# Two-layer decoder trunk on one core: the second layer's latents as seven half-size products, and the sums of the fourth product of the last projection made ahead of its splits

## The chip, the core and the metric

The kernel runs on one core of a Trainium2 chip. The metric is device time in microseconds (us) for one execution of the whole program, lower is better. The kernel before has a median of 718.78 us over 3 runs (718.22 to 719.83). Engines are named as in the profile: PE is TensorE (PEld its weight loads), ACT is ScalarE, DVE is VectorE, POOL is GpSimd, SP is SyncE, which here only issues DMAs.

## The reference

512 tokens of width 1024 go through two layers and a last norm. What matters here is the second layer (multi-head latent attention):

```python
def mla_layer(x, cos, sin, norm_g, w_in, q_norm_g, w_q_b, kv_norm_g, w_kv_b, w_out):
    h = rmsnorm(x, norm_g)
    proj = h @ w_in                       # 512 x 1024 times 1024 x (384 + 256 + 64 + 2048)
    q_lat, kv_lat, k_rope, z = proj[..., :o1], proj[..., o1:o2], proj[..., o2:o3], proj[..., o3:]
    q = (rmsnorm(q_lat, q_norm_g) @ w_q_b).reshape(B, S, N_HEADS, QK_HEAD_DIM)
    kv = (rmsnorm(kv_lat, kv_norm_g) @ w_kv_b).reshape(B, S, N_HEADS, QK_NOPE_DIM + V_HEAD_DIM)
...
    o = causal_mla_attention(q_nope, q_rope, k_nope, k_rope, v)
    y = o.reshape(B, S, MLA_WIDTH) * jax.nn.silu(z)
    return x + y @ w_out                  # 512 x 2048 times 2048 x 1024
```

All is float32. The first 704 columns of proj (384 + 256 + 64) are called the latents here; the other 2048 feed the gates, silu(z).

## The kernel before

**Arithmetic.** A float32 product is made of three fast ones: every operand is split into a high half (`w_hi`, `h_hi`, `a_hi`: ScalarE copies it into the type fp32r) and a low half (what is left; VectorE or GpSimd subtracts). `mm3` (lines 183 to 185) multiplies high by high, low by high and high by low into one bank of PSUM. So each strip of weights costs a pass of ScalarE and then a pass of VectorE (or GpSimd) before TensorE can use it. `halves` (188, 189) does this for data, `strip` (166, 167) for weights loaded into five `raw` buffers, `Summed.strip` (559, 560) for weights that stand in tiles of their own. Halves of weights live in four buffers (`WB = 4`, tag "w"), so two strips at a time. PSUM has eight banks, given out by `bank()`.

**Seven products for eight.** Both output projections cut their matrices into two by two quarters and multiply by a scheme of Strassen's kind: seven products of sums of quarters take the place of eight. `x_sum` and `y_sum` hold sums of weight quarters, made by loads (some of them adding loads of GpSimd's queue); `s1`, `s2`, `s3`, `n3` are sums of token quarters, made by VectorE (`combine`, `combine_rows`, line 1055). `multiply` runs one product: two strips (q) by two tiles of 128 tokens (t), each of them `part`, 12 matmuls. `gather` (610) adds a bank to the residual `xs`.

**Around the latents.** The last product of the first layer's projection goes tile by tile; `norm_a` and `norm_b` (226: transposes through PSUM, then halves) make the second layer's normed tokens `h_hi`, `h_lo`, feature major. `lat_block(i, t)` then makes the latents without any scheme: two halves of 352 columns by two halves of the 1024 features (four strips, low halves on GpSimd) by four token tiles, 12 matmuls each. A bank is copied to `lat` (706). After that `latents()` norms them (rms of the 384 and of the 256 columns), and `gates(0)` to `gates(7)`, 48 matmuls of 512 columns each, run with the transposes of the latents, the rope of the keys and of the first queries between them.

**Order.** Here and in the attention the framework's planner sets the order of each engine's queue: an instruction that the program writes first goes first, unless its model of the work says that another is ready earlier; a tile of memory is handed on when its last reader is done. At the start and in the last projection, under `tc.manual_schedule()`, each engine takes its instructions in the order in which the program writes them.

**The last projection** (`products`, `finish`): seven products over `a11` to `a22`, quarters of `y`. Before `products`, the attention's last heads run the first one (into `acc`) and prepare the second. In `products`: second product (`t1`, into `both`), third (`p2`, into `last`), fourth (`y1` by `n3`, into `both`), fifth (`t2` by `s2`, into `acc`), sixth (`y2` by `s3`), and in `finish` the seventh (`t4` by `a22`).

## Time and profile before

| | |
|---|---|
| median of 3 runs | 718.78 us (718.22 to 719.83) |
| the profiled execution's own time | 719.61 us |
| its span, first to last instruction | 717.8 us |
| mean granted TensorE clock | 0.991 |
| instructions | 10049, of them 3529 matmuls |
| latents, starts of the first and the last matmul of 352 columns | 313.12 and 345.49 us |
| gates(0), starts of its first and last matmul | 345.65 and 356.33 us |
| last projection: second product starts, kernel ends | about 639 us, 717.8 us |

How to read the profile: times are from the start of the span. In the timeline a row is start, duration, engine, line, operation, written tile<-read tiles, shape and count; in brackets stands how long the engine was idle before it and what released it. A matmul's duration holds its way through the array, so the rate is read from the distance between starts. In the list of waits a row is who waited, for whom, total us, times, longest. Groups by shape give count, then busy us and mean ns of one. "Granted clock" is TensorE's share of its full clock.

## The change

**The latents.** `norm_b` gets a third argument: it turns both halves of a token tile first, makes the halves, and then ScalarE also copies the plain values from PSUM into `hf`, the upper half of the tile `y`, which the gates fill only later. `lat_block` gives way to `latent_products`: tokens are cut into two halves of 256, features into two halves of 512, columns into two of 352. Four quarters of weights are loaded into tiles of their own (`w_q`, eight loads of 352 KB) and added in place by VectorE; token sums are made in place in `hf`; seven products of 24 matmuls are accumulated in six banks and read out to `lat` by ScalarE and VectorE with the signs that the scheme asks. All low halves of these strips are VectorE's. `gates(0)` moves from behind the latents to between the second and the third product; `latents` (the norm) follows the products, and `gates(1)` stands where `gates(0)` stood, and so on.

**The last projection.** The third product's second strip moves up, ahead of two sums and of the two reads of `acc`; all of `n3` is summed before its first split; the two strips of the fourth product are written apart with the second split of `n3` between them; the reads of `acc` come after them.

```diff
-    def norm_b(t, xn):
-        for b in range(2):
-            pt = bank()
+    def norm_b(t, xn, plain=None):
+        pts = [bank() for _ in range(2)]
+        for b, pt in enumerate(pts):
...
+        if plain is not None:
+            for b, pt in enumerate(pts):
+                o = plain[:, 4 * b : 4 * b + 4, t * P : (t + 1) * P]
+                act.activation(o, pt.rearrange("p (k c) -> p k c", k=4), AF.Copy)
...
-    lat_block(0, 0)
-    norm_b(2, xn[2])
-    lat_block(0, 1)
-    lat_block(1, 0)
-    norm_b(3, xn[3])
-    for i, t in ((1, 1), (0, 2), (0, 3), (1, 2), (1, 3)):
-        lat_block(i, t)
-    for i in (2, 3):
-        for t in range(NT):
-            lat_block(i, t)
...
+        def form(raw):
+            hi = wp.tile([P, W], F32R, name="w_hi", tag="w", bufs=WB)
+            lo = wp.tile([P, W], F32R, name="w_lo", tag="w", bufs=WB)
+            hv, lv = (t[:, : 4 * HL].rearrange("p (k c) -> p k c", k=4) for t in (hi, lo))
+            for k in (slice(0, 2), slice(2, 4)):
+                halves(raw[:, k, :], hv[:, k, :], lv[:, k, :])
+            return hv, lv
+
+        def add(a, b):
+            for k in (slice(0, 2), slice(2, 4)):
+                dve.tensor_tensor(a[:, k, :], a[:, k, :], b[:, k, :], ALU.add)
...
+        p1 = form(b11)
+        times(acc, p1, tokens(0, 0), True, 0)
+        norm_b(2, xn[2], hf)
+        times(acc, p1, tokens(0, 0), True, 1)
+        p2 = form(b21)
+        times(last, p2, tokens(0, 1), True, 0)
+        norm_b(3, xn[3], hf)
+        times(last, p2, tokens(0, 1), True, 1)
+        add(b11, b12)
+        gates(0)
+        dve.tensor_tensor(a22, a21, a22, ALU.subtract)
+        s1 = a_form(a22, "one")
+        for t in range(2):
+            act.activation(lat[:, t, cl], acc[t][:, cols], AF.Copy)
+        both = [bank() for _ in range(2)]
+        t1 = form(b11)
+        product(both, t1, s1, True)
+        dve.tensor_tensor(a21, a11, a21, ALU.subtract)
+        dve.tensor_tensor(a11, a22, a11, ALU.subtract)
+        add(b11, b22)
+        s2 = a_form(a11, "two")
+        t2 = form(b11)
+        for t in range(2):
+            dve.tensor_tensor(lat[:, t, cl], lat[:, t, cl], last[t][:, cols], ALU.add)
+            act.activation(lat[:, 2 + t, cr], both[t][:, cols], AF.Copy)
+        product(acc, t2, s2, False)
+        dve.tensor_tensor(a12, a11, a12, ALU.add)
+        n3 = a_form(a12, "one")
+        y1 = form(b22)
+        for t in range(2):
+            act.activation(lat[:, t, cr], acc[t][:, cols], AF.Copy, scale=-1.0)
+        product(both, y1, n3, False)
+        add(b12, b22)
+        s3 = a_form(a21, "two")
+        y2 = form(b12)
+        for t in range(2):
+            dve.tensor_tensor(lat[:, t, cr], lat[:, t, cr], both[t][:, cols], ALU.add)
+        product(acc, y2, s3, False)
+        add(b11, b21)
+        t4 = form(b11)
+        for t in range(2):
+            c = lat[:, 2 + t, cr]
+            dve.tensor_tensor(c, c, acc[t][:, cols], ALU.subtract)
+        for t in range(2):
+            times(acc, t4, tokens(1, 1), False, t)
+            act.activation(lat[:, 2 + t, cl], acc[t][:, cols], AF.Copy)
...
         split_rows(a12, slots[1], 4, 8)
+        p2.append(y_sum.strip(1))
         combine_rows(s3, a11, a21, ALU.subtract, 6, 8)
         combine_rows(s2, s1, a11, ALU.subtract, 6, 8)
-        for t in range(2):
-            gather(t, LEFT, acc[t])
-        p2.append(y_sum.strip(1))
         y_sum.load(1, RIGHT)
         multiply(last, p2, slots[1], True)
         n3 = a12
-        combine_rows(n3, s2, a12, ALU.add, 0, 4)
+        combine_rows(n3, s2, a12, ALU.add, 0, 8)
         split_rows(n3, slots[0], 0, 4)
-        combine_rows(n3, s2, a12, ALU.add, 4, 8)
-        split_rows(n3, slots[0], 4, 8)
         for t in range(2):
             gather(2 + t, RIGHT, both[t])
-        y1 = y_sum.strips()
+        y1 = [y_sum.strip(0)]
+        split_rows(n3, slots[0], 4, 8)
+        y1.append(y_sum.strip(1))
+        for t in range(2):
+            gather(t, LEFT, acc[t])
```

## What was predicted, before the change was built

> **What bounds the kernel now.** I read the page first (shares, chain), then TensorE's list of waits, then a table of stages, then the timeline of the two places that the change touches.

> ```profile
> PE 701.5 (98%) x3529; PEld 600.8 (84%) x3529; DVE 444.5 (62%) x866; ACT 347.2 (48%) x748; POOL 138.0 (19%) x182
> ...
> PE 93%; DVE 3%; issue 1%; ACT 1%; DMA 0%; POOL 0%; POOLq 0%; SPq 0%; DVEq 0%; ACTq 0%
> ```

> TensorE is busy 98% of the span and carries 93% of the chain that ended last. So time falls only by fewer matmuls or fewer waits of TensorE.

> ```profile
> PE bank L183 <- ACT w_hi L559: 2.5, 1, 2.5
> ...
> PE bank L226 <- DVE xn L218: 0.6, 1, 0.6
> PE bank L185 <- DVE w_lo L560: 0.5, 1, 0.5
> ```

> Those are TensorE's only waits of 0.5 us or more once the first products run. The one of 0.6 us is for the second layer's norm and stays; the other two belong to the strips of the last projection.

> ```profile
> 313.00:357.00 44.00, 44.00 (x263) 41.71 (x261) 18.77 (x44) 23.02 (x59) 23.89 (x35) 1.00 0.40 111
> ...
> 660.40:670.30 9.90, 6.89 (x17) 4.64 (x16) 8.98 (x9) 6.57 (x7) 4.86 (x4) 0.66 0.31 50
> ```

> The columns are the stretch, its length, then busy time of PE, PEld, DVE, ACT and POOL, the granted clock, and DMA. The latents with gates(0) (313 to 357) have no idle PE, with VectorE at 18.77 of 44. Around 660 PE idles, and the clock is 0.66. The timeline shows it:

> ```profile
> 650.00 0.39 PE L184 MATMUL bank<-w_hi,a_lo 128*128 128x512 f32 x1
> ...
> 660.42 0.39 PE L185 MATMUL bank<-w_lo,a_hi 128*128 128x512 f32 x1
> 663.29 0.69 PE L183 MATMUL bank<-w_hi,a_hi 128*128 128x512 f32 x1 [2.48 <-ACT w_hi L559]
> 663.78 0.63 PE L184 MATMUL bank<-w_hi,a_lo 128*128 128x512 f32 x1
> 664.94 0.80 PE L185 MATMUL bank<-w_lo,a_hi 128*128 128x512 f32 x1 [0.52 <-DVE w_lo L560]
> ...
> 669.80 0.58 PE L184 MATMUL bank<-w_hi,a_lo 128*128 128x512 f32 x1
> 670.22 0.39 PE L185 MATMUL bank<-w_lo,a_hi 128*128 128x512 f32 x1
> ```

> From 650.00 to 660.42 lie 47 matmuls, 46 steps of 0.2265 us. From 660.42 to 670.22 there are 15 steps, 9.80 us; at 0.2265 they would be 3.40. The hole costs **6.40 us**: about 2.6 us of wait, 0.5 of a second one, and some 3.3 because the matmuls up to 669.80 come 0.43 us apart, at half clock, until it recovers.

> **Part 1, the latents: matmuls.** Before: 16 blocks of 12, 192 matmuls of 352 columns. After: seven products of 24, 168.

> ```profile
> 321.34 0.32 PE L183 MATMUL bank<-w_hi,h_hi 128*128 128x352 f32 x1
> ...
> 345.49 0.32 PE L185 MATMUL bank<-w_lo,h_hi 128*128 128x352 f32 x1
> ```

> This run has 153 rows, 152 steps: 0.1589 us each. The 24 that go are worth **3.81 us**. [...]

> **Part 1: what the seven products ask of VectorE.** Low halves of the strips now run on VectorE, and VectorE adds weights and tokens. Rows for the rates:

> ```profile
> 338.11 2.20 ACT L166 ACTIVATE w_hi<-raw 128x512 fp32r<-128x512 f32 x4 [5.13 <-PE bank L184]
> 661.20 3.88 ACT L559 ACTIVATE w_hi<-b_y 128x1024 fp32r<-128x1024 f32 x4
> 671.19 0.63 ACT L1219 ACTIVATE junk<-xs 128x512 f32<-128x512 f32 x1 [4.22 <-DVE xs L610]
> ...
> 671.94 0.63 ACT L1219 ACTIVATE junk<-xs 128x512 f32<-128x512 f32 x1
> 338.78 2.50 DVE L167 TENSOR_TENSOR w_lo<-raw,w_hi 128x512 fp32r<-128x512 f32 x4 [16.24 <-ACT w_hi L166]
> 663.66 4.62 DVE L560 TENSOR_TENSOR w_lo<-b_y,w_hi 128x1024 fp32r<-128x1024 f32 x4
> ```

> and, from the groups by shape in 313 to 357 (count, then busy us and mean ns):

> ```profile
> L189 DVE TENSOR_TENSOR h_lo<-bank,h_hi 128x512 fp32r<-128x512 f32 x5 | 3.3, 685 | 0.2 <-ACT h_hi L188 0.2
> L218 DVE SCALAR_TENSOR_TENSOR xn<-xs,rs,g_mla 128x1024 f32<-128x1024 f32 x2 | 2.6, 1285 | 4.6 <-POOL rs L204 4.6
> ...
> L610 DVE TENSOR_TENSOR xs<-xs,bank 128x512 f32<-128x512 f32 x1 | 0.7, 678 | 0.0
> ```

> Per operation in a row: VectorE 0.625 us at 512 columns, 1.155 at 1024, so 0.82 for the new shape of 704 (between those rows); ScalarE 0.55, 0.97 and so 0.71; a square with its sum takes 0.75. From the first product's start (313.1) to the last one's start VectorE has: 6 strips, two pieces each (9.8 us); the gates(0) strip (2.5); 4 weight sums of two pieces (6.6); 4 token sums (4.6); 4 low halves of tokens (4.6); 6 bank reads of 352 columns at some 0.46 (by the slope of the two rows; 0.625 at most), 2.8; and what it has already, 3.3 + 2.6 + 0.7. Sum 37.5 us. TensorE in the same stretch: 6 products (22.9), gates(0), 48 x 0.2265 = 10.9, and two norm transposes:

> ```profile
> 315.05 1.04 PE L226 MATMUL bank<-ident,xn 128*128 128x128 f32 x8
> 315.84 0.41 PE L183 MATMUL bank<-w_hi,h_hi 128*128 128x352 f32 x1
> ```

> 0.8 us each. Sum 35.4. VectorE's 37.5 drops by 2.2 for what is not in the way (one bank read, the last strip's second piece, the part of a norm that ran ahead of 313.1): 35.3 against 35.4. It is now as loaded as TensorE. Worked through in program order, gates(0) lets it make the sums for the next two products ahead; afterwards each product has 3.8 us of cover against 4.0 to 5.4 us of VectorE work, and TensorE is reached about the end. ScalarE's high halves must come first (0.71 for each piece), and strips wait for one of two pairs of weight buffers, free when the product before the last one ends. I take **1.0 us** of waits in all; bounds: 0 (every sum made ahead) and 4 (VectorE never idle in the sum above, but waiting about 0.8 us for ScalarE at each of five products). Below nothing it cannot go, since this stretch has no idle PE to win back. Latents net: 1.0 - 3.8 = **-2.8 us**.

> **At nothing.** The eight plain copies of the norm (ScalarE, 0.55 each) lie where ScalarE has 21 of 44 us free; uncovered, two would hold a norm's banks 1.1 us longer. gates(0) only moves: gates(1), 10.9 us, takes over hiding the latents' norm and the rows of it; the projection loads of gates(0) are queued on SP behind eight loads of quarter weights, which need memory of the first layer's last strips:

> ```profile
> 302.21 2.35 DVE L560 TENSOR_TENSOR w_lo<-b_x,w_hi 128x1024 fp32r<-128x1024 f32 x2
> ...
> raw<-in_mla_w_in SPq DMA_DIRECT2D x16, 176.0 KB, 2.5
> ```

> free by 304.6 at the latest; 352 KB at twice the 2.5 us are there by 310, and TensorE wants the product at 313.1. If that cover went, 2 to 3 us. GpSimd loses 16 low halves; nobody waited for them.

> **Part 2, the fourth product's operands.** What made the hole, in order on ScalarE and VectorE:

> ```profile
> 649.74 2.01 ACT L559 ACTIVATE w_hi<-b_y 128x1024 fp32r<-128x1024 f32 x2 [0.98 <-PE bank L184]
> 656.62 1.06 ACT L188 ACTIVATE a_hi<-y 128x1024 fp32r<-128x1024 f32 x1 [4.86 <-DVE y L1055]
> 660.23 1.06 ACT L188 ACTIVATE a_hi<-y 128x1024 fp32r<-128x1024 f32 x1 [2.56 <-DVE y L1055]
> ...
> 649.37 1.22 DVE L189 TENSOR_TENSOR a_lo<-y,a_hi 128x1024 fp32r<-128x1024 f32 x1
> 655.29 1.29 DVE L1055 TENSOR_TENSOR y<-y 128x512 f32<-128x512 f32 x2
> 657.71 1.23 DVE L189 TENSOR_TENSOR a_lo<-y,a_hi 128x1024 fp32r<-128x1024 f32 x1 [1.13 <-ACT a_hi L188]
> 658.85 1.29 DVE L1055 TENSOR_TENSOR y<-y 128x512 f32<-128x512 f32 x2
> 662.47 1.28 DVE L610 TENSOR_TENSOR xs<-xs,bank 128x512 f32<-128x512 f32 x2
> ```

> The second half of the sum waits on VectorE behind a low half that waits for ScalarE; ScalarE's queue then holds the strip (661.20) behind that sum's high half (660.23). New order: third product's second strip, low, from its first high half at 650.8 to 653.1; two sums to 654.4; all four pieces of n3 (0.64 each) to 657.0. ScalarE: first half of n3 from 655.7, at worst from 657.0; strip of y1 done by 658.6, at worst 659.9. VectorE: low half to 658.1, two reads of banks to 659.4, y1's first piece to 660.6. TensorE wants high halves at 660.65 and the first low at 661.1: no wait, 0.5 us to spare. Then n3's rest to 662.9 and y1's second strip to 665.2, wanted at 666.1. The moved reads of acc end at 666.5, s2's low halves 668.8, last's reads 670.1. ScalarE squares these (0.75 each) to 670.95, and only then takes the fifth product's strip: first high 671.5, first low 672.1; wanted 671.5 and 672.0. I keep 0.2 us of wait there: **-6.2 us**. Loads:

> ```profile
> b_y<-in_mla_w_out SPq DMA_DIRECT2D x4, 512.0 KB, 6.0
> ```

> y1's are issued as p2's low halves end (648.3 to 653.1) and wanted from 656.7 to 661.8, 8.4 us or more later, 6.0 needed. GpSimd's adding loads go earlier with them.

> Sum: 719.61 - 2.8 - 6.2 = 710.6 for a profiled execution; that one lies 0.83 above the median, which gives **709.8**.

> **Rivals.** (a) The forecast, 709.8: 0.63. (b) VectorE's load costs the latents all they save, in waits under 2 us each: 718.8 - 6.2 = 712.6. For it: 35.3 against 35.4; against: GpSimd's part is gone, and gates(0) lets work run ahead. 0.14. (c) The hole only moves to the fifth product, behind the squares (0.1 us to spare): 2.5 us of wait and the half clock are back, 718.8 - 2.8 = 716.0. 0.11. It needs 2 us of lateness that my queue does not have. (d) The half clock after the hole is not in every run. The lowest time is only 1.39 below the profiled one, so at most that much of 3.3 us is absent; the median gains 1.2 less: 711.0. 0.05. [...] (e) Slower: in the latents the sums queue behind each other so that two of the five late products wait 2.5 us or more. The hole shows the price of such a wait, 6.4 us with the clock: 718.8 - 10.0 + 12.8 = 721.6. It decides from 2.5 us on; for it, t2's step is 7.7 us of VectorE (two token sums, a weight sum, two low halves, two bank reads) against 3.8 of cover if gates(0) did not help. 0.05. No change within the bound: 0.02. That the change does not do as it says I see no room for: seven calls, one order written by hand.

> **How the numbers follow.** Low end: no waits (-3.8 - 6.4) and 0.6 of scatter: 708.0. High end: (a), (b), (d) and (b) with 2 us more, 714.8; (c) and (e) left out, 0.16 to 0.18. About 0.2% (1.4 us) is what a measurement here can tell from no change. Faster: a to d, 0.93, less 0.02 for mixtures: 0.91; same 0.04; slower 0.05.

> **What would show it.** Right: no wait of PE for the strip's high half near 660, clock 1.0 there, matmuls 0.2265 apart; 168 matmuls of 352 columns 0.159 apart; VectorE near full from 313 to 349; PE waits there of about 1 us in sum. Wrong: PE waits of 2 us or a clock below 1 among the products, or a new hole at the squares.

## The result, and the profile after

The change's median is 711.67 us over 4 runs (711.33 to 712.01), against 718.79 for the kernel before, run beside it. The ratio is 0.9896, with a 95% interval of 0.9884 to 0.9908. Its profiled execution took 712.01 us (span 710.2, clock 0.992), 7.60 less than that of before. Timed again later it gave 711.06 (710.38 to 711.35), 0.9882 (0.9869 to 0.9895). The forecast was 709.8, so the direction and the range held and the gain came out 1.9 us smaller.

From the page of the changed kernel, the engines' busy time and the shares of the chain:

```profile
PE 696.8 (98%) x3505; PEld 596.5 (84%) x3505; DVE 474.0 (67%) x902; ACT 358.4 (50%) x758; POOL 126.2 (18%) x166
...
PE 94%; DVE 2%; issue 1%; ACT 1%; POOL 1%; DMA 1%; POOLq 0%; SPq 0%; DVEq 0%; ACTq 0%
```

TensorE runs 24 matmuls less and is still the bound. Its list of waits, without those of the first 10 us:

```profile
PE bank L226 <- DVE xn L218: 0.9, 2, 0.6
PE bank L183 <- ACT h_hi L188: 0.4, 1, 0.4
PE bank L185 <- DVE h_lo L189: 0.4, 1, 0.4
```

The 2.5 us for the strip's high half and the 0.5 behind it are gone. Three waits are new: one of 0.3 for a norm (the 0.9 holds two waits, and the other, of 0.6, was there before), and two of 0.4 that name the halves of normed tokens. None names a strip of the late products. The windows of the two places (stretch, length, busy PE, PEld, DVE, ACT, POOL, granted clock, DMA):

```profile
313.00:353.00 40.00, 38.85 (x224) 35.85 (x223) 37.14 (x49) 28.13 (x54) 7.62 (x12) 1.00 0.13 41
...
651.00:662.00 11.00, 11.00 (x50) 9.13 (x49) 10.97 (x14) 6.53 (x7) 2.42 (x2) 1.00 0.63 212
```

VectorE, at 18.77 of 44 before, is now busy 37.14 of 40 in the latents, and PE has about 1.2 us without work there. Where the hole was, PE is full at clock 1.00. The timeline of the same place, the step into the fourth product:

```profile
659.12 0.39 PE L185 MATMUL bank<-w_lo,a_hi 128*128 128x512 f32 x1
659.35 0.39 PE L183 MATMUL bank<-w_hi,a_hi 128*128 128x512 f32 x1
659.58 0.39 PE L184 MATMUL bank<-w_hi,a_lo 128*128 128x512 f32 x1
659.80 0.39 PE L185 MATMUL bank<-w_lo,a_hi 128*128 128x512 f32 x1
```

The matmul of 659.12 is the third product's last and that of 659.35 the fourth's first; starts lie 0.22 to 0.23 apart across the step. The first low half was ready in time:

```profile
657.90 2.35 DVE L564 TENSOR_TENSOR w_lo<-b_y,w_hi 128x1024 fp32r<-128x1024 f32 x2
```

The first of its two pieces ends about 659.1, and the matmul that wants it starts at 659.80: 0.7 us to spare, where the prediction had 0.5.

**Where the 7.60 us are**, from starts of matmuls in the two profiled executions. The first matmul of 352 columns comes 0.63 later (313.12, then 313.75); the first one of 512 columns does too (26.31, then 26.93), so this was there before any line of the change had run, and 712.01 is the highest of the four runs. From the first 352-column matmul to the first transpose of the latents' rows, gates(0) and gates(1) both counted: 54.31, now 52.34, so 1.97 less. From there to the last product's last high matmul: 342.97, now 336.73, so 6.24 less. What is left is 0.02.

## The experiments

The table has those two stretches for each kernel's profiled execution ("latents", "after them"; gates(1), 48 x 0.2265 = 10.87 us, moved into the first where it stands later), beside the times. Ratios are against the kernel before, timed beside each.

| kernel | median us | ratio (95%) | latents | after them |
|---|---|---|---|---|
| before | 718.79 | 1 | 54.31 | 342.97 |
| the change | 711.67 | 0.9896 (0.9884 to 0.9908) | 52.34 | 336.73 |
| last projection only | 712.82 | 0.9923 (0.9910 to 0.9937) | 54.30 | 336.73 |
| latents only | 716.76 | 0.9973 (0.9959 to 0.9987) | 52.35 | 342.11 |
| two strips' low halves on GpSimd | 712.59 | 0.9924 (0.9909 to 0.9938) | 54.20 | 336.70 |
| plain copy first | 709.74 | 0.9881 (0.9866 to 0.9897) | 51.35 | 336.72 |
| reads of acc where they were | 710.65 | 0.9893 (0.9875 to 0.9911) | 52.35 | 336.89 |
| n3 by halves in turn | 714.42 | 0.9942 (0.9924 to 0.9960) | 52.35 | 339.65 |
| 8 spare sums | 717.87 | 0.9988 (0.9977 to 0.9999) | 58.69 | 336.72 |
| 4 spare sums | 713.01 | 0.9923 (0.9900 to 0.9945) | 54.13 | 336.98 |
| the change, again | 711.06 | 0.9882 (0.9869 to 0.9895) | 52.33 | 336.66 |
| plain copy first, again | 710.21 | 0.9873 (0.9859 to 0.9887) | 51.35 | 336.68 |
| no plain copies | 711.98 | 0.9903 (0.9885 to 0.9921) | 52.12 | 336.69 |

The stretches repeat to 0.1 us in kernels that don't differ in them, but for the 4 spare sums, whose second stretch is 0.3 longer. The medians of one kernel differ more from one timing to the next: 0.5 for the plain copy first, 0.6 for the change, and up to 1.6 for the kernel before (718.16 to 719.77). So small differences are read from the stretches.

**The two halves of the change, each alone.** The kernel before with the last projection's lines of the change:

```diff
...
-        combine_rows(n3, s2, a12, ALU.add, 0, 4)
+        combine_rows(n3, s2, a12, ALU.add, 0, 8)
         split_rows(n3, slots[0], 0, 4)
-        combine_rows(n3, s2, a12, ALU.add, 4, 8)
-        split_rows(n3, slots[0], 4, 8)
...
-        y1 = y_sum.strips()
+        y1 = [y_sum.strip(0)]
+        split_rows(n3, slots[0], 4, 8)
+        y1.append(y_sum.strip(1))
...
```

> The kernel before with the new order of the last projection alone. My theory: the hole ahead of the fourth product goes with its half clock and nothing is late behind it, so the span falls by 6.3 us (second product's first matmul to the last matmul 64.9 us in place of 71.2), the median by 5.5 to 6.4 us, since the length of the half clock may differ from run to run. Rival, that the hole moves on to the fifth product (the squares): a wait of 2 us or more there, and under 3.5 us gained. Rival, that the two parts only work together: the times of this run and of the latents alone do not add up to the 7.1 us of both.

and the change with the last projection of before (the same lines the other way round):

> The change's latents alone, with the last projection in the order of before. My theory: 24 matmuls fewer are worth 3.8 us, and waits at the second tile's norm and at the start of the gates give 1.7 back, so the median falls by 1.4 to 2.2 us and the hole ahead of the fourth product with its half clock is there as before (about 6.4 us). Rival, that the seven products of the latents cost all they save: within 0.5 us of before.

By the medians -5.3 and -1.4, in sum -6.7, and -7.1 together: the halves add up to within the scatter of the medians. By the stretches -6.24 and -1.96, the same as in the change. With the latents alone the hole is there, as in the kernel before:

```profile
658.43 0.39 PE L185 MATMUL bank<-w_lo,a_hi 128*128 128x512 f32 x1
661.30 0.47 PE L183 MATMUL bank<-w_hi,a_hi 128*128 128x512 f32 x1 [2.48 <-ACT w_hi L563]
```

and the clock falls behind it, in two windows with PE alone (stretch, length, busy PE, granted clock, DMA):

```profile
659.83:663.24 3.41, 1.01 (x3) 1.00 0.00 0
663.24:666.65 3.41, 3.41 (x9) 0.50 0.44 54
```

The same wait of 2.48 us, and a second one of 0.94. The half clock lasts 3.41 us here, from 663.24 to 666.65; before it lasted 6.82, from 663.38 to 670.20. The hole costs 5.4 here (342.11 against 336.73) and 6.2 there.

**Which edit closed the hole.** The change with n3 summed and split half by half again:

```diff
-        combine_rows(n3, s2, a12, ALU.add, 0, 8)
+        combine_rows(n3, s2, a12, ALU.add, 0, 4)
         split_rows(n3, slots[0], 0, 4)
+        combine_rows(n3, s2, a12, ALU.add, 4, 8)
+        split_rows(n3, slots[0], 4, 8)
...
-        split_rows(n3, slots[0], 4, 8)
```

> The change with n3 summed and split by halves in turn, as before (the strip and the reads stay as changed), so ScalarE's queue holds the fourth product's strip behind n3's second high half, which waits for VectorE. My theory: this turn-taking made the hole. TensorE waits 0.5 to 1 us for the high half and 1.5 to 2.5 us for the low half; if the clock stays whole the time is 2 to 3.5 us above the change's, if a wait of this length halves it, 4 to 6.5 us above. Rival (the strip's place made the hole, and the sums do not matter): within 0.5 us of the change.

and the change with the third product's second strip and the reads of `acc` in their old places:

```diff
-        p2.append(y_sum.strip(1))
         combine_rows(s3, a11, a21, ALU.subtract, 6, 8)
         combine_rows(s2, s1, a11, ALU.subtract, 6, 8)
+        for t in range(2):
+            gather(t, LEFT, acc[t])
+        p2.append(y_sum.strip(1))
...
-        for t in range(2):
-            gather(t, LEFT, acc[t])
```

> The change with one of the three edits of the last projection undone: the third product's second strip and the two reads of acc stand as before, so VectorE has 1.3 us more ahead of the fourth product's first low half. My theory (the working of the prediction: 0.5 us to spare there): TensorE waits about 0.8 us for that low half, once, the clock stays whole, and the time is 0.5 to 1.2 us above the change's. Rival (any wait there brings the half clock back): 3 us or more above the change. Rival (the reads do not matter): same within 0.3 us.

These two old places cost 0.16 us in the stretch and nothing in the time, where 0.5 to 1.2 was expected: the first low half came 0.8 us later, not 1.3, and there were 0.7 to spare, not 0.5, so the matmul that wants it starts 0.2 us late (659.67). The turn-taking of n3 costs 2.92, and 0.46% by the ratios, 3.3 us. Its TensorE:

```profile
658.42 0.39 PE L185 MATMUL bank<-w_lo,a_hi 128*128 128x512 f32 x1
660.43 0.47 PE L183 MATMUL bank<-w_hi,a_hi 128*128 128x512 f32 x1 [1.63 <-ACT w_hi L563]
660.74 0.40 PE L184 MATMUL bank<-w_hi,a_lo 128*128 128x512 f32 x1
662.07 0.50 PE L185 MATMUL bank<-w_lo,a_hi 128*128 128x512 f32 x1 [0.94 <-DVE w_lo L564]
662.41 0.40 PE L183 MATMUL bank<-w_hi,a_hi 128*128 128x512 f32 x1
```

2.0 us pass between two starts instead of 0.23, then 1.3; after that the matmuls are at full speed, 0.23 between starts. So n3's order made most of the waiting; the time is as expected with a whole clock, though the longer of the two waits is that for the high half. With the other two moves kept, the first wait is 1.63 instead of 2.48 us, and the clock holds. The 2.92 and the 0.16 are only half of the 6.24: the rest, most of it half clock, was seen only with all three old places together. The last section shows why the clock may have held here by luck.

**The waits in the latents: the plain copies.** In the change's ScalarE timeline:

```profile
304.00 1.07 ACT L188 ACTIVATE h_hi<-bank 128x512 fp32r<-128x512 f32 x2
307.87 1.20 ACT L232 ACTIVATE y<-bank 128x512 f32<-128x512 f32 x2 [2.80 <-DVE h_lo L189]
308.96 1.46 ACT L188 ACTIVATE w_hi<-w_q 128x704 fp32r<-128x704 f32 x2
310.78 1.09 ACT L188 ACTIVATE h_hi<-bank 128x512 fp32r<-128x512 f32 x2 [0.35 <-PE bank L226]
312.11 1.06 ACT L198 ACTIVATE xn<-xs 128x1024 f32<-128x1024 f32 x1 [0.24 <-DVE xs L614]
...
321.01 1.20 ACT L232 ACTIVATE y<-bank 128x512 f32<-128x512 f32 x2 [1.25 <-DVE h_lo L189]
```

ScalarE stands idle 2.80 us ahead of the plain copy (L232), until VectorE has made the low half from the same bank. Both only read the bank, and here they took turns: of the two low halves (307.15, 1.28 us for both) the first ends about 307.8, and the copy starts at 307.87. What makes the copy wait for another reader was not shown. Behind the copy stand the first strip's high halves (308.96), and behind these VectorE:

```profile
309.78 1.69 DVE L189 TENSOR_TENSOR w_lo<-w_q,w_hi 128x704 fp32r<-128x704 f32 x2 [1.35 <-ACT w_hi L188]
311.39 0.68 DVE L614 TENSOR_TENSOR xs<-xs,bank 128x512 f32<-128x512 f32 x1
...
314.84 1.28 DVE L218 SCALAR_TENSOR_TENSOR xn<-xs,rs,g_mla 128x1024 f32<-128x1024 f32 x1 [0.77 <-POOL rs L204]
```

The residual of the third token tile (311.39) waits behind the low halves, its square on ScalarE (312.11) behind it, and its norm is made at 314.84. TensorE has this to show for it:

```profile
315.51 0.32 PE L185 MATMUL bank<-w_lo,h_hi 128*128 128x352 f32 x1
316.17 1.09 PE L226 MATMUL bank<-ident,xn 128*128 128x128 f32 x8 [0.34 <-DVE xn L218]
...
324.30 0.50 PE L183 MATMUL bank<-h_hi,w_hi 128*128 128x512 f32 x1 [0.41 <-ACT h_hi L188]
...
325.43 0.50 PE L185 MATMUL bank<-h_lo,w_hi 128*128 128x512 f32 x1 [0.40 <-DVE h_lo L189]
```

Between starts 0.50, 0.57 and 0.57 are lost at these three, and about 0.1 at each restart. The last two are at gates(0), whose strip and the fourth tile's halves queue behind another copy that waits 1.25 us (321.01). If that is the cause, the copy should be written ahead of the low half:

```diff
-        pts = [bank() for _ in range(2)]
-        for b, pt in enumerate(pts):
+        for b in range(2):
+            pt = bank()
...
-            halves(pt.rearrange("p (k c) -> p k c", k=4), h_hi[o], h_lo[o])
-        if plain is not None:
-            for b, pt in enumerate(pts):
-                o = plain[:, 4 * b : 4 * b + 4, t * P : (t + 1) * P]
-                act.activation(o, pt.rearrange("p (k c) -> p k c", k=4), AF.Copy)
+            src = pt.rearrange("p (k c) -> p k c", k=4)
+            act.activation(h_hi[o], src, AF.Copy)
+            if plain is not None:
+                act.activation(plain[o], src, AF.Copy)
+            dve.tensor_tensor(h_lo[o], src, f32(h_hi[o]), ALU.subtract)
```

> The change with each plain copy of the norm written ahead of VectorE's low half of the same bank, in place of after it, so that ScalarE does not wait for VectorE there; the work is the same. Theory A (ScalarE's queue stands still at the plain copies, 2.8 and 1.25 us of idle, and the strip of the first product, the gates' strip and the last tile's high halves stand behind them): the waits at the third tile's transposes and at the gates go for the most part, 1.0 to 1.7 us less than the change. Theory B (VectorE's load as such): no gain, since VectorE has the same work; within 0.3 us of the change, or slower by up to 0.5 us since each low half starts 0.6 us later.

Its ScalarE no longer waits for VectorE there:

```profile
303.20 0.59 ACT L231 ACTIVATE y<-bank 128x512 f32<-128x512 f32 x1
303.68 0.60 ACT L229 ACTIVATE h_hi<-bank 128x512 fp32r<-128x512 f32 x1
304.16 0.61 ACT L231 ACTIVATE y<-bank 128x512 f32<-128x512 f32 x1
306.16 1.48 ACT L188 ACTIVATE w_hi<-w_q 128x704 fp32r<-128x704 f32 x2 [1.39 <-issue]
```

The wait for the third tile's norm is gone, the latents take 1.0 us less (51.35), and the ratio falls to 0.9881. Beside the change on one chip:

> The change itself, unaltered, on the chip of the two runs that it is compared with here: 711.7 by its earlier runs.

> The kernel in which the plain copy of a transposed half is written ahead of VectorE's low half of the same bank, timed once more beside the change. If the 1.0 us by which its stretch of the latents was shorter in the profile is a gain of every run: 1.0 to 1.1 us below the change here too. If it was the scatter of one chip: within 0.4 us of the change.

710.21 (709.73 to 710.47) against 711.06: 0.85 us less by the medians, with intervals of the ratios that overlap, and once more 51.35 against 52.33 in the stretch. The times alone don't tell the two apart; the stretch does, twice. This is the fastest kernel of the case. The attempt to price the copies by leaving all eight out (the sums of tokens are then made from other data):

```diff
-        if plain is not None:
+        if plain is not None and False:
```

> The eight plain copies of the transposed norms left out, so that the sums of tokens for the second layer's latents are made from other data. If the copies cost only by the wait for VectorE's low half: as the kernel with the plain copies first, within 0.3 us, since there two waits of 0.5 and 0.2 us are left whose releasers are the norm of tile 3 and a low half. If the copies cost ScalarE's time as well: another 0.5 to 0.8 us below that kernel. If they cost nothing, as the prediction had it: as the change.

It was as the change (711.98; 52.12 in the stretch), but it says nothing of the copies. Freed from them, the planner put sums of tokens ahead of the norms on VectorE:

```profile
301.22 1.22 DVE L781 TENSOR_TENSOR y<-y 128x1024 f32<-128x1024 f32 x1
303.21 1.28 DVE L218 SCALAR_TENSOR_TENSOR xn<-xs,rs,g_mla 128x1024 f32<-128x1024 f32 x1 [0.77 <-POOL rs L204]
```

so the norm was late in another way. The first product began 288.33 us after the first 512-column matmul instead of 286.82; 0.7 us of that is lost at the norms, and 0.8 already near 280 us, at a low half of the first layer whose load (`b_y`) landed later in this execution. That run is inconclusive on what the copies cost.

**Is VectorE too full?** The low halves of the first two strips went back to GpSimd:

```diff
...
-        p1 = form(b11)
+        p1 = form(b11, pool)
...
-        p2 = form(b21)
+        p2 = form(b21, pool)
```

> The change with the low halves of the first two strips of the latents' weights on GpSimd, as all four strips had it before. Theory A (the waits come from the norm's steps, which stand in the queues of VectorE and ScalarE behind these strips and behind the plain copies): the wait of the third tile's transposes (0.5 us) goes, that at the gates in part; 0.5 to 1.0 us less than the change. Theory B (VectorE's load as such makes the waits, wherever they show): both waits go, 1.5 us or more less than the change. Theory C (the waits have another cause): same as the change within 0.3 us.

A miss: the latents take 1.9 us more, not less. GpSimd's timeline in that kernel:

```profile
308.17 3.38 POOL L189 TENSOR_TENSOR w_lo<-w_q,w_hi 128x704 fp32r<-128x704 f32 x2 [3.91 <-ACT w_hi L188]
311.64 0.75 POOL L203 TENSOR_SCALAR rs<-ssq 128x1 f32<-128x1 f32 x1
312.47 0.57 POOL L204 TENSOR_TENSOR rs<-rs,mhalf 128x1 f32<-128x1 f32 x1
313.01 4.34 POOL L189 TENSOR_TENSOR w_lo<-w_q,w_hi 128x704 fp32r<-128x704 f32 x2
```

and VectorE's:

```profile
310.37 1.94 DVE L733 TENSOR_TENSOR w_q<-w_q 128x704 f32<-128x704 f32 x1
313.07 2.72 DVE L218 SCALAR_TENSOR_TENSOR xn<-xs,rs,g_mla 128x1024 f32<-128x1024 f32 x1 [0.77 <-POOL rs L204]
```

While GpSimd subtracts, VectorE's norm takes 2.72 us, 1.28 in the change, and its weight sum 1.94, elsewhere 0.88; the norm's factor rs is GpSimd's as well and queues with the low halves. TensorE then waits 1.66 us for the third tile's norm. GpSimd's piece of 313.01 ends at 314.71 and the norm 1.1 us after it, about the 1.28 that a norm takes alone, and GpSimd's next piece takes 2.69 us where the other three take 1.70. What makes the two slower beside each other was not shown. So the low halves of these two strips are better left with VectorE. How much room it has there was measured by sums that nobody reads:

```diff
             for k in (slice(0, 2), slice(2, 4)):
                 dve.tensor_tensor(a[:, k, :], a[:, k, :], b[:, k, :], ALU.add)
+                if k.start < 4:
+                    spare = lw.tile([P, 2, HL], F32, name="spare", tag="spare", bufs=1)
+                    dve.tensor_tensor(spare, a[:, k, :], b[:, k, :], ALU.add)
```

> The change with each of the eight pieces of the latents' weight sums written once more into a tile that nobody reads: 8 x 0.8 = 6.4 us more of VectorE between the first and the last product. The prediction's ledger (VectorE 35.3 us against TensorE's 35.4, so no slack): waits at the late products of 5 us or more in all. Rival (the late products have slack that the ledger did not see: the trace has their low halves ready 0.7 to 1.2 us ahead): part of it is hidden, 1 to 4 us above the change.

> As the run with eight spare sums, but only the first piece of each sum is written once more: 4 x 0.8 = 3.2 us more of VectorE. Ledger without slack: 2.5 us or more above the change. Slack of 0.7 to 1.2 us at each late product: within 1.2 us of the change, and less than half of what eight spare sums cost.

(the second with `k.start < 1`). Four sums of 0.80 us, 3.2, made the stretch 1.79 longer, so 1.4 of them were free. Eight, 6.4, made it 6.35 longer, and there the clock fell after the waits at the late products:

```profile
347.82 0.32 PE L184 MATMUL bank<-w_hi,a_form 128*128 128x352 f32 x1
348.84 0.43 PE L185 MATMUL bank<-w_lo,a_form 128*128 128x352 f32 x1 [0.70 <-DVE w_lo L189]
...
352.00 0.32 PE L185 MATMUL bank<-w_lo,a_form 128*128 128x352 f32 x1
354.36 0.73 PE L183 MATMUL bank<-h_hi,w_hi 128*128 128x512 f32 x2 [2.04 <-ACT w_hi L166]
355.75 0.66 PE L183 MATMUL bank<-w_hi,h_hi 128*128 128x352 f32 x1 [0.66 <-DVE lat L800]
356.20 0.49 PE L184 MATMUL bank<-w_hi,h_lo 128*128 128x352 f32 x1
...
359.14 0.33 PE L185 MATMUL bank<-w_lo,h_hi 128*128 128x352 f32 x1
```

From 355.75 to 359.14 stand 11 steps, 3.39 us; at 0.1589 they would be 1.75. So 1.6 of the 6.35 are clock, 4.7 are waits, and 1.7 of the 6.4 were free. Neither run meets one of its two expectations in full: four sums cost 1.8 (2.5 or more, or under 1.2, was expected), and eight made 4.7 of waits (5 or more) in 6.35 (1 to 4). About 1.5 us of added VectorE work found room, with one caveat: the longest wait, 2.04 us here and 1.23 with four sums, is that of gates(1), two matmuls of which the planner put ahead of the last product once the sums were there (in both kernels). With four sums only one late product waits, 0.19 us, so the products alone may have more room; that was not measured.

## Why the prediction was right, and where it was off

**Part 2** stood, term for term: -6.2 said, -6.24 measured, no wait, clock 1.00, starts 0.2265 apart. The 0.2 us kept for the fifth product did not come, and the 0.5 us to spare at the first low half was 0.7. Of its three moves n3's order counted most: undone alone it brings back 2.92 us of waits, without the half clock; the other two bring back 0.16. That the size fits to 0.04 us is partly luck: it was read from one execution of the kernel before, and the same hole costs 5.4 us in the execution with the latents only.

**Part 1, the matmuls**: 168 of them, 0.159 apart, 3.81 less, as said.

**Part 1, the waits** is the step that was mis-sized: "I take 1.0 us of waits in all". The net was -1.97 instead of -2.8, so the waits took 1.84 (3.81 less 1.97); the three gaps above are 1.64 of them. They are not where it put them. VectorE's load was priced well: it was busy 35.42 of the 37.45 us from the first product's start to the last one's. But no late product waits at all; some 1.5 us more work found room there, not the 0.1 of "35.3 against 35.4". All waits are at the norms of the third and fourth tiles and at gates(0).

**"At nothing: the eight plain copies"** is what failed behind that. It priced a copy by ScalarE's free time and bounded it by the bank held longer. It did not ask what the copy waits for (VectorE's low half of the same bank, 2.80 us) nor who stands behind it on ScalarE (the first strip, the next tile's square). With the copy first, 1.0 us of the loss is gone; the rest is waits of 0.5 and 0.2 between starts, for the fourth tile's norm and a low half. At that norm GpSimd's step L204 takes 1.06 us, 0.57 at the other tiles, while VectorE adds weights; that is about the 0.5. The 0.2 was not taken apart.

**"GpSimd loses 16 low halves; nobody waited for them"** was true of the kernel before and not the whole: when four of the pieces were given back, VectorE's norm took 2.72 us beside them instead of 1.28, and TensorE waited 1.66 us for it.

**The sum.** 710.6 was said for a profiled execution, 712.01 measured: +0.83 for the latents, -0.04 for the last projection, +0.63 for the start of that execution, -0.02 left. It lies 0.34 above its median, where 0.83 was taken over from before, another 0.49; together the 1.9 us. So 0.8 of the 1.9 is the mis-sized term, and the rest is scatter between executions. The high end of the range, 714.8, is 0.2 more than its own sum (712.6 and 2); nothing hangs on it.

**The rivals.** The result lies between (a), 709.8, and (b), 712.6: waits ate 1.8 of the 3.8 us saved, not all. (c), the hole moved on, and (e), late products waiting 2.5 us, did not happen; the run with eight spare sums shows (e)'s mechanism with its price, 1.6 us of clock on top of the waits, and that the clock, whole with 3.2 us of added VectorE work, fell with 6.4, though the longest wait there is at gates(1). (d): last projection only gains 5.3 by the median, 4.5 to 6.5 by its interval, so 6.2 in every run is not excluded, nor a little less. Its mechanism was seen: the half clock lasted 6.82 us in one profiled execution and 3.41 in the other, and the hole cost 0.9 less there. The kernel with the latents alone also scatters more (714.06 to 717.91 over 12 runs; the change 711.33 to 712.01 and 710.38 to 711.35, over 4 each), and of its 12 runs the two with the highest mean clock, 0.997, took 714.06 and 714.15, the five with the lowest, 0.990, 716.77 to 717.91. That the length of the half clock makes this scatter is still argued, not shown: the kernel without plain copies, which hasn't the hole, scatters from 710.89 to 715.28 over 6 runs.

## What to carry to other kernels

An instruction put on an idle engine was free here only where it could start when its turn came (one copy left ScalarE idle for 2.80 us): ask what it waits for and what stands behind it, before asking how much time the engine has left. Two engines that read one bank took turns here, so the reader that others queue behind should go first: put first, it took 1.0 us off the latents. Sums made ahead of all splits, instead of in turn with them, kept two engines here from waiting for each other by halves, worth 2.92 us.

## What the runs showed of the hardware that was not expected

```profile
659.97:663.38 3.41, 0.93 (x5) 1.00 0.01 3
663.38:666.79 3.41, 2.89 (x6) 0.50 0.00 0
666.79:670.20 3.41, 3.41 (x9) 0.50 0.87 139
...
656.58:659.99 3.41, 2.23 (x10) 1.00 0.03 11
659.99:663.41 3.42, 2.04 (x8) 1.00 0.00 0
...
352.31:355.72 3.41, 0.74 (x3) 1.00 0.00 0
355.72:359.13 3.41, 3.38 (x11) 0.50 0.02 5
```

In these three kernels and in the one with the latents only, the clock fell behind windows in which PE was busy 0.74 to 1.01 us, and held behind 2.04 and 2.23. It stayed at half behind 2.89 (the second wait lies in that window) and came back behind 3.38 and 3.41. With n3 by halves PE waits 1.63 and 0.94 us, 2.57 in all, about what the latents only idle in one window (2.4), but the edge at 659.99 divides it. Whether the clock falls in another execution of that kernel was not seen. The windows did not stand at one place of the program: the rise lies 11.47 us ahead of the first 512-column matmul in the kernel before and 11.02 in the change, which are not a whole number of windows apart.

The first 512-column matmul, whose program text is the same in all thirteen profiled executions, started from 25.03 to 26.93 us after the span's start in them. In four of them (both with the plain copy first, the old reads, no plain copies) another 0.3 to 0.8 us is lost near 280 us, where loads of `b_y` landed later. So 2 us and more between two single executions can come from before the part that was edited.
